# Hyena's tiles over n1 read four and two ahead, begun after a longer delay, with a larger share of the merge

## The chip, the core and the metric

One core of one Trainium2 chip runs the whole program. The metric is device time of one execution in microseconds. The core has five engines with queues of their own: PE (matmuls, with PEld for its weight loads), DVE, ACT, POOL and SP. SP does no arithmetic here; it issues nearly all DMAs, one after another.

## The reference, cut to what matters

Two sequences (512 and 2048 rows of width 1024) go through one layer of an encoder. Its inner width is divided into three branches: an mLSTM, a retention and a Hyena. The Hyena branch is what the change touches:

```python
def long_conv(u, spec, skip):
    l = u.shape[1]
    y = jnp.fft.irfft(jnp.fft.rfft(u, n=2 * l, axis=1) * spec[None], n=2 * l, axis=1)[:, :l]
    return y + u * skip

def hyena_branch(hy_in, hy_z, conv_w, conv_b, spec, skip):
    u = centred_conv3(hy_in.astype(f32), conv_w.astype(f32), conv_b.astype(f32))
    v, x1, x2 = u[..., :HY_WIDTH], u[..., HY_WIDTH:2 * HY_WIDTH], u[..., 2 * HY_WIDTH:]
    z = x1 * long_conv(v, spec[:, 0], sk[0])
    z = x2 * long_conv(z, spec[:, 1], sk[1])
    return z * jax.nn.silu(hy_z.astype(f32))
```

## The kernel before, in words

**Stages.** `front` normalises the rows, and starts the projections and the Hyena filters. Then one merge runs two streams side by side: the Hyena chain `stage_a0`, `freq(0)`, `inv_a(0)`, `freq(1)`, `inv_a(1)`, and the chain `projections`, `retention`. Then come `mlstm` and `final`.

**The Hyena chain.** A long convolution is a Fourier transform split in two steps, over n1 and over n2. `stage_a` is the step over n1: two matmuls (line 921) on one tile read from DRAM (`X`, line 790), two copies on ACT (924) and two stores into `Sg` (925). `stage_a0` does it for 20 tiles (4 of the short sequence, 16 of the long one). `freq(o)` is the step over n2 for 20 pairs of frequencies: matmuls of lines 948 and 983, products on DVE and POOL, results into `Z`. `inv_a(o)` is the inverse step over n1, 20 tiles again. Its `load` reads two tiles of `Z` (line 890), `load_x` reads a tile of the second factor `X` (and for o = 1 a tile of the gate `hyg`) in two halves of 64 partitions each (790), `mid` does two matmuls (1028), a product on DVE (1029) and, for o = 1, a product on POOL (1033) and two stores into `ymix` (1036). For o = 0 `back` passes the product to `stage_a` instead. All these tiles come from one pool, `hb`, of 18 buffers of 128x512 f32 (256 KB).

**The order.** Each stream is a Python generator that emits instructions and yields `(cost, due, pe)`. `merge` takes, of the streams that are due, the one with the smallest sum of costs divided by its weight; `self.now` moves on by the PE cost. `lag(cost, lag)` says that the stream isn't due again before its own cost and `lag` more have gone by. So a weight sets the share, and a lag holds a stream back at least so long. The sums are in planned us. The program is built with `schedule_with_timeline_sim=True`: the framework takes the emitted order as the priority, and from a model of time of its own settles the order of each engine's queue, in which one instruction may pass another. On the chip each queue then runs in that order.

**Beside it.** Line 544 is the projection of Hyena and mLSTM columns, line 554 that of retention and of gates; 376 to 378, 675, 680 and 693 make the filters; 1681 to 1702 and 1639 are retention. `RtHead` of head 3 is the last of the second stream. `before_mlstm` splits the first weights of the mLSTM; line 512 reads weights, line 348 takes their maximum on DVE.

Of the kernel before, what the change touches and what calls it, by code (L numbers as in the profile page):

```python
# [38 lines left out]
LF, LA, LI, LT, W1, W2, W3, LN, LM = 2.7, 1.0, 4.2, 1.6, 0.8, 1.08, 1.03, 1.5, 3.5  # L39
# [4 lines left out]
def geo(L):  # L44
    N = 2 * L
    N1 = N // 64
    V = N1 // 2
    return dict(N=N, N1=N1, K1=N1 // 2, V=V, GF=128 // N1, GS=128 // V, NTF=N // 128, NTS=L // 128)
# [105 lines left out]
class Trunk:  # L154
# [62 lines left out]
    def run(self):  # L217
        tc = self.tc
        with ExitStack() as ctx:
            self.psum = ctx.enter_context(tc.tile_pool(name="psum", bufs=8, space=PSUM))  # L220
            self.dram = ctx.enter_context(tc.tile_pool(name="dram", bufs=1, space=DRAM))
            self.cp = ctx.enter_context(tc.tile_pool(name="cp", bufs=1))
            self.setup()
            with ExitStack() as c1:
                self.hp = c1.enter_context(tc.tile_pool(name="hp", bufs=1))
                self.wp = c1.enter_context(tc.tile_pool(name="wp", bufs=2))
                self.hT = [[self.T(self.hp, [128, 8, 512], "h", F16, bufs=10) for i in range(2)] for b in range(5)]
                self.filter_pool = ExitStack()
                self.drain(self.front())
                with tc.tile_pool(name="hy", bufs=2, side="right") as self.hy:  # L230
                    self.load_ai()
                    self.drain(self.merge((self.chain(self.stage_a0(), self.freq(0), self.inv_a(0), self.freq(1), self.inv_a(1)), 275 * W3),
                                          (self.chain(self.projections(), self.retention()), 848)))
                self.drain(self.mlstm())
                with tc.tile_pool(name="fin", bufs=2, **TW) as self.fin:
                    self.final()
# [659 lines left out]
    def stage_a0(self):  # L896
        seq = [(L, j) for L in (LP, LS) for j in range(geo(L)['NTS'])]
        st = {}

        def load(i):  # L900
            L, j = seq[i]
            st[i] = self.hx(0, L, j)

        n = len(seq)
        load(0)
        load(1)
        for i in range(n + 1):
            if i:
                L, j = seq[i - 1]
                self.stage_a(L, 0, j, st.pop(i - 1))  # L910
            if i + 2 < n:
                load(i + 2)
            yield self.lag(0.86, 1.5)

    def stage_a(self, L, o, j, t):
        nc = self.nc
# [92 lines left out]
    def inv_a(self, o):  # L1009
        nc = self.nc  # L1010
        seq = [(L, j) for L in ((LS, LP), (LP, LS))[o] for j in range(geo(L)['NTS'])]
        zs, xs, st = {}, {}, {}

        def load(i):
            L, j = seq[i]
            zs[i] = [self.hb(self.Z[L, o][:, geo(L)['NTS'] * h + j::2 * geo(L)['NTS'], :]) for h in range(2)]

        def load_x(i):
            L, j = seq[i]
            g = self.in_halves(self.half_rows(self.hyg, L, j)) if o == 1 else None  # L1020
            xs[i] = self.hx(o + 1, L, j), g

        def mid(i):
            L, j = seq[i]
            z, (x, g) = zs.pop(i), xs.pop(i)
            ps = self.ps()
            for h in range(2):
                nc.tensor.matmul(ps[64 * h:64 * h + 64], self.ai[L][:, 128:192], z[h], start=True, stop=True)  # L1028
            nc.vector.tensor_tensor(out=x, in0=x, in1=ps, op=ALU.mult)
            if o == 0:  # L1030
                st[i] = x
            else:
                nc.gpsimd.tensor_tensor(out=g, in0=g, in1=x, op=ALU.mult)
                rows = self.half_rows(self.ymix[:, 1024:1536], L, j)
                for h in range(2):
                    nc.sync.dma_start(rows[h], g[64 * h:64 * h + 64])

        def back(i):
            L, j = seq[i]
            self.stage_a(L, 1, j, st.pop(i))  # L1040

        n = len(seq)
        load(0)
        yield self.lag(0.0, 5.0)
        for i in range(-1, n + 1):
            if o == 0 and i >= 1:
                back(i - 1)
            if 0 <= i < n:
                mid(i)
            if i + 1 < n:  # L1050
                load_x(i + 1)
            if i + 2 < n:
                load(i + 2)
            yield self.lag(1.71 if o == 0 else 0.86, LI)

    def gates(self):
        nc, I, tc = self.nc, self.I, self.tc
# [678 lines left out]
```

## Time and profile before

| | |
|---|---|
| time, median of 3 runs | 2651.07 us (2650.94 to 2654.84) |
| the profiled execution | 2648.68 us, span 2646.9 us |
| PE busy | 2557.2 us, 97% of the span |
| DVE, ACT, POOL busy | 51%, 40%, 19% |
| DMA | 321 MB, 39.8% of the 16 engines' time on SP's queue |
| mean granted TensorE clock | 0.988 |

PE is busy nearly all the time, so what can be won lies in the few stretches where it waits or where its clock is halved (a granted clock of 0.5 is 1.2 GHz, 1.0 is 2.4 GHz). An instruction's start is given from the span's start.

### The profile page before, as it was taken

To read this page: it belongs to the slowest core of one execution; us is meant where nothing else is said; L and a number is where in the kernel's file an instruction comes from. 1 tells how busy PE (TensorE), PEld (TensorE's weight loads), DVE (VectorE), ACT (ScalarE), POOL (GpSimd) and SP (SyncE) were. 2 spreads that over 40 slices of the span, in tenths; PEclk is the share of its full clock that TensorE was granted. 3 is DMA by queue.
4 is the path that set the end of the run, shared out by engine and by line. 5 is a ranking of instruction groups with operands and counts; after the bars stand their busy time and mean duration, and the time that the engine had idled before them with its cause. 6 is when DMAs were issued, how large, how long until landed. Compare 5 with 4: busy or idle time off the path is not lost.

```text
span 2646.9 us, 45607 instructions
## 1 busy us (share of the span) xinstructions
PE 2557.2 (97%) x17830; PEld 1770.2 (67%) x17830; DVE 1338.3 (51%) x3070; ACT 1053.7 (40%) x2030; POOL 493.9 (19%) x647
## 2 busy tenths in 40 slices
PE   7999979999999999999999979999999999899998
PEld 5565543444446777777777747787887777788887
DVE  6875635665554434545444444565556645522222
ACT  6455646442233333423333323555445545411111
POOL 0103312331011122322232341111111111100000
PEclk9999989999999999999999989999999999999999
DMA  6233377564454665434333782222121322322331
GB/s 207 84 99 108 98 220 252 167 187 127 126 160 128 207 198 160 126 100 132 116 104 97 226 228 65 52 66 61 37 64 42 89 73 59 133 102 95 111 104 48
DMA packets 238049, 321.30 MB, mean 121 GB/s; under 512 B 22755, under 2 KB 125947, under 8 KB 237833
## 3 DMA queue, kind: packets, MB, share of 16 engines
q1 hardware_dynamic: 237752, 318.11, 39.8%
q8 instruction: 141, 2.31, 0.4%
q14 instruction: 76, 0.61, 0.1%
q0 software_dynamic: 80, 0.26, 0.0%
HBM read 205.41 MB, written 112.89 MB: 120 GB/s over the span
## 4 chain that ended last, share of the span: by engine, by line
PE 78%; DMA 6%; ACT 4%; DVE 4%; issue 1%; SPq 1%; POOL 1%; DVEq 0%; POOLq 0%; ACTq 0%
PE ps L554 27%; PE ps L544 13%; PE ps L1287 13%; PE ps L948 6%; DMA rb<-rowd 3%; PE ps L983 3%; PE ps L1028 2%; PE ps L921 1%; PE ps L1639 1%; DMA wraw<-in_w_in 1%; PE ps L693 1%; PE ps L1438 1%; PE ps L1275 1%; PE ps L1698 1%; PE ps L846 1%
## 5 line engine op out<-in xcount | busy, mean ns | idle before, releaser
L554 PE MATMUL ps<-whi,h 128*128 128x256 f16 (+2 forms) x6080 | 913.7, 256 | 0.0
L554 PEld LDWEIGHTS <-h 128*128 128x128 f16 x9120 | 776.0, 98 | 150.0 <-issue 69.5
L554 PE MATMUL ps<-wlo,h 128*128 128x256 f16 (+2 forms) x3040 | 734.6, 256 | 0.0
L544 PE MATMUL ps<-h,whi 128*128 128x512 f16 x1600 | 484.9, 383 | 4.0 <-ACT whi L526 4.0
L544 PE MATMUL ps<-h,wlo 128*128 128x512 f16 x800 | 305.0, 381 | 0.0
L544 PEld LDWEIGHTS <-whi 128*128 128x128 f16 x1600 | 151.1, 99 | 212.8 <-issue 63.0
L1287 PE MATMUL ps<-h,yh 128*128 128x512 f32 x760 | 210.6, 396 | 1.6 <-ACT yh L369 1.6
L948 PE MATMUL ps<-hb,cB 128*64 128x512 f32 x640 | 165.9, 605 | 0.2 <-DMA hb<-F 0.2
L1287 PEld LDWEIGHTS ps<-h,yh 128*128 128x128 f32 x760 | 141.6, 188 | 33.7 <-ACT yh L369 1.9
L668 POOL TENSOR_TENSOR acc<-acc,win 128x512 f32<-128x512 f32 x80 | 107.2, 1340 | 201.4 <-ACT win L667 196.2
L544 PEld LDWEIGHTS <-wlo 128*128 128x128 f16 x800 | 78.7, 98 | 94.7 <-issue 4.9
L1618 POOL TENSOR_TENSOR m<-raw,tb 128x256 f32<-128x256 f32 x80 | 72.3, 904 | 336.2 <-ACT raw L1615 273.2
L1287 PE MATMUL ps<-h,yl 128*128 128x512 f32 x380 | 120.9, 395 | 0.0
L1615 ACT ACTIVATE raw<-ps,winv 128x256 f32<-128x256 f32 x80 | 37.8, 473 | 167.5 <-PE ps L554 98.9
L662 DVE TENSOR_TENSOR f<-ps,win 128x512 f32<-128x512 f32 x80 | 55.0, 688 | 88.7 <-PE ps L378 66.1
L813 DVE SCALAR_TENSOR_TENSOR cv<-u,sw,cv 128x512 f32<-128x512 f32 x120 | 98.1, 838 | 1.1
L527 DVE SCALAR_TENSOR_TENSOR wlo<-wraw,wsc,whi 128x512 f16<-128x512 f32 (+2 forms) x116 | 82.6, 749 | 22.8 <-ACT whi L526 21.6
L1637 ACT ACTIVATE vw<-va,rtv 128x128 f32<-128x128 f32 x144 | 51.9, 398 | 100.4 <-PE ps L1639 100.0
L948 PEld LDWEIGHTS ps<-hb,cB 128*64 128x64 f32 x640 | 41.5, 136 | 73.2 <-issue 60.6
L348 DVE TENSOR_REDUCE wam<-wraw 128x1 f32<-128x2048 f32 (+2 forms) x29 | 60.0, 2069 | 60.0 <-DMA wraw<-in_w_in 60.0
L1343 DVE TENSOR_TENSOR xt<-xt,ps 128x512 f32<-128x512 f32 x40 | 25.8, 684 | 126.9 <-PE ps L1287 126.9
L971 POOL TENSOR_TENSOR hb<-hb,hb 128x512 f32<-128x512 f32 x40 | 50.9, 1273 | 185.5 <-DVE hb L970 176.3
(318 smaller groups left out, 4045.8 us busy)
## 6 DMA issues: line engine op xcount, KB each, us to landing
F<-fo SPq DMA_DIRECT2D x160, 128.0 KB, 2.4
Sg<-hb SPq DMA_DIRECT2D x80, 256.0 KB, 2.3
hb<-F SPq DMA_DIRECT2D x80, 256.0 KB, 4.3
hb<-Sg SPq DMA_DIRECT2D x80, 256.0 KB, 5.1
Z<-hb SPq DMA_DIRECT2D x80, 256.0 KB, 3.5
hb<-Z SPq DMA_DIRECT2D x80, 256.0 KB, 3.7
rb<-rowd SPq DMA_DIRECT2D x80, 256.0 KB, 5.1
wraw<-in_w_in SPq DMA_DIRECT2D x36, 512.0 KB, 5.8
```

Source lines behind the costliest of these rows:

```text
L348: self.nc.vector.tensor_reduce(am[:, 0:1], src, axis=AX.XY if len(src.shape) == 3 else AX.X, op=ALU.max, apply_absolute_value=True)
L527: v = nc.vector.scalar_tensor_tensor(lo[:, k], raw[:, k], s, hi[:, k], op0=ALU.mult, op1=ALU.subtract)
L544: nc.tensor.matmul(out, w[x][:, k, wc:wc + 128], self.hT[b][y][:, k], start=(k == 0 and i == 0), stop=(k == 7 and i == 2))
L554: nc.tensor.matmul(out, self.hT[b][x][:, k, c * 128:(c + 1) * 128], w[y][:, k, wc:wc + n], start=(k == 0 and i == 0), stop=(k == 7 and i = ...
L662: nc.vector.tensor_tensor(out=f, in0=ps, in1=win, op=ALU.mult)
L668: nc.gpsimd.tensor_tensor(out=acc, in0=acc, in1=win, op=ALU.add)
L813: nc.vector.scalar_tensor_tensor(d, u[:, t:t + 512], w(t), d, op0=ALU.mult, op1=ALU.add)
L948: nc.tensor.matmul(ps[half[h]], Cs[i][:, 128 * h + 64 * r:128 * h + 64 * r + 64], src[h], start=True, stop=True)
L983: nc.tensor.matmul(pz[h], c[half[h], 256 + 128 * r:384 + 128 * r], y[r][half[h]], start=(r == 0), stop=(r == 1))
L1028: nc.tensor.matmul(ps[64 * h:64 * h + 64], self.ai[L][:, 128:192], z[h], start=True, stop=True)
L1287: self.nc.tensor.matmul(self.pss[n], a[p], w[q][:, n * 512:(n + 1) * 512], start=(k == 0 and i == 0), stop=(k == 11 and i == 2))
L1618: nc.gpsimd.tensor_tensor(out=m, in0=raw[:, :, ::-1], in1=sin[:, c:c + 2], op=ALU.mult)
```

## The change

The Hyena's weight in the merge goes from 275 to 295 (times 1.03). `stage_a0` reads four tiles before the first and stays four ahead (before: two), is first due after 9.0, and its tiles cost 1.0 with a lag of 0.5 (before: 0.86 and 1.5). `inv_a` reads two whole tiles first, `Z` and the factors, stays two ahead with both (before: `Z` two ahead, the factors one), is first due after 7.0 (before: 5.0 and then an empty round of its own cost and lag), and its tiles cost 1.0 or 2.0 with a lag of 1.5 (before: 0.86 or 1.71 with 4.2). In a round of `inv_a(0)` `mid` and the loads now come ahead of `back`. No instruction is added or taken out.

```diff
-  self.drain(self.merge((self.chain(self.stage_a0(), self.freq(0), self.inv_a(0), self.freq(1), self.inv_a(1)), 275 * W3),
+  self.drain(self.merge((self.chain(self.stage_a0(), self.freq(0), self.inv_a(0), self.freq(1), self.inv_a(1)), 295 * W3),
                         (self.chain(self.projections(), self.retention()), 848)))
...
         n = len(seq)
-        load(0)
-        load(1)
-        for i in range(n + 1):
-            if i:
-                L, j = seq[i - 1]
-                self.stage_a(L, 0, j, st.pop(i - 1))
-            if i + 2 < n:
-                load(i + 2)
-            yield self.lag(0.86, 1.5)
+        for i in range(4):
+            load(i)
+        yield self.lag(0.0, 9.0)
+        for i in range(n):
+            L, j = seq[i]
+            self.stage_a(L, 0, j, st.pop(i))
+            if i + 4 < n:
+                load(i + 4)
+            yield self.lag(1.0, 0.5)
...
         n = len(seq)
-        load(0)
-        yield self.lag(0.0, 5.0)
-        for i in range(-1, n + 1):
+        for i in range(2):
+            load(i)
+            load_x(i)
+        yield self.lag(0.0, 7.0)
+        for i in range(n + 1):
+            if i < n:
+                mid(i)
+            if i + 2 < n:
+                load(i + 2)
+                load_x(i + 2)
             if o == 0 and i >= 1:
                 back(i - 1)
-            if 0 <= i < n:
-                mid(i)
-            if i + 1 < n:
-                load_x(i + 1)
-            if i + 2 < n:
-                load(i + 2)
-            yield self.lag(1.71 if o == 0 else 0.86, LI)
+            yield self.lag(1.0 if o else 2.0, 1.5)
```

## Rows read from the trace of the kernel before

**Rows 1.** Windows by stage: length, PE, PEld, DVE, ACT, POOL busy, clock, DMA, GB/s

```profile
362.00:456.00 94.00, 83.18 (x354) 34.17 (x358) 43.15 (x71) 51.04 (x88) 17.78 (x25) 0.91 0.75 241
456.00:872.00 416.00, 414.68 (x2574) 200.78 (x2567) 222.39 (x430) 151.29 (x265) 82.17 (x124) 1.00 0.51 152
872.00:1019.00 147.00, 147.00 (x1099) 104.05 (x1098) 60.71 (x159) 59.28 (x134) 33.24 (x32) 1.00 0.66 208
1019.00:1465.00 446.00, 445.06 (x3365) 323.06 (x3366) 207.90 (x522) 151.41 (x338) 125.31 (x114) 1.00 0.36 113
...
1540.00:1567.00 27.00, 22.65 (x123) 13.38 (x122) 15.00 (x33) 6.21 (x16) 12.89 (x11) 0.94 0.83 235
1567.00:1592.00 25.00, 13.95 (x31) 3.65 (x31) 4.22 (x14) 1.50 (x4) 4.79 (x4) 0.73 0.65 182
```

**Rows 2.** PE's timeline where the merge begins: start, us, instruction, idle before

```profile
353.57 0.61 PE L544 MATMUL ps<-h,whi 128*128 128x512 f16 x2
...
358.55 0.38 PE L544 MATMUL ps<-h,wlo 128*128 128x512 f16 x1
367.07 3.78 PE L921 MATMUL ps<-hb,ai 64*128 64x512 f32 x8 [8.14 <-DMA hb<-X]
370.78 1.02 PE L675 MATMUL ps<-acc,ones 128*1 128x512 f32 x2
371.73 1.05 PE L680 MATMUL ps<-ones,acc 128*128 128x1 f32 x8
372.71 1.13 PE L921 MATMUL ps<-hb,ai 64*128 64x512 f32 x4
...
386.48 0.80 PE L376 MATMUL ps<-w,hd 128*128 128x512 f32 x1 [4.11 <-ACT w L369]
```

**Rows 3.** SP's timeline there: issues of DMAs

```profile
362.64 0.83 SPq L779 DMA_DIRECT2D ai<-c_AI  x2
363.51 3.81 SPq L790 DMA_DIRECT2D hb<-X  x6
```

**Rows 4.** PE's waits from 1540 to 1592

```profile
PE ps L1028 <- DMA hb<-Z: 11.1, 3, 4.8
PE ps L1700 <- DVE cf L1643: 2.9, 1, 2.9
PE ps L1698 <- DVE pt L1691: 0.8, 1, 0.8
PE ps L1689 <- ACT qkT L1682: 0.7, 1, 0.7
```

**Rows 5.** PE's timeline at the end of the merge

```profile
1550.11 1.88 PE L1028 MATMUL ps<-hb,ai 128*64 128x512 f32 x4
...
1553.44 1.07 PE L1028 MATMUL ps<-hb,ai 128*64 128x512 f32 x2
...
1560.24 1.08 PE L1028 MATMUL ps<-hb,ai 128*64 128x512 f32 x4
1561.67 1.08 PE L1028 MATMUL ps<-hb,ai 128*64 128x512 f32 x4
...
1563.99 1.07 PE L1028 MATMUL ps<-hb,ai 128*64 128x512 f32 x2
...
1566.86 0.49 PE L1700 MATMUL ps<-cf,qw 128*128 128x128 f32 x2
1570.53 1.73 PE L1028 MATMUL ps<-hb,ai 128*64 128x512 f32 x4 [3.19 <-DMA hb<-Z]
1577.06 3.44 PE L1028 MATMUL ps<-hb,ai 128*64 128x512 f32 x4 [4.80 <-DMA hb<-Z]
1583.57 1.94 PE L1028 MATMUL ps<-hb,ai 128*64 128x512 f32 x2 [3.06 <-DMA hb<-Z]
...
1591.11 1.07 PE L1028 MATMUL ps<-hb,ai 128*64 128x512 f32 x2
```

**Rows 6.** Windows: all of 1471 to 1540 and 1465 to 1567, then line 1028 alone

```profile
1471.00:1540.00 69.00, 69.00 (x550) 53.18 (x548) 37.81 (x83) 22.76 (x58) 34.49 (x29) 1.00 0.86 248
...
1465.00:1567.00 102.00, 97.65 (x725) 71.92 (x723) 55.03 (x121) 31.21 (x78) 48.32 (x42) 0.98 0.84 242
...
1465.00:1540.00 75.00, 12.94 (x44) 2.36 (x44) 1.00 0.85 245
```

**Rows 7.** SP's timeline in the last stage, 1471 to 1540: first, some, last

```profile
1471.59 2.17 SPq L790 DMA_DIRECT2D hb<-X  x2
...
1475.42 0.45 SPq L790 DMA_DIRECT2D hb<-hyg  x1
1476.68 1.10 SPq L1036 DMA_DIRECT2D ymix<-hb  x2
1477.84 0.59 SPq L790 DMA_DIRECT2D hb<-hyg  x1
1478.48 1.24 SPq L790 DMA_DIRECT2D hb<-X  x2
1479.76 1.06 SPq L890 DMA_DIRECT2D hb<-Z  x2
1480.92 1.09 SPq L790 DMA_DIRECT2D hb<-hyg  x2
1482.11 1.18 SPq L1036 DMA_DIRECT2D ymix<-hb  x2
...
1538.44 3.65 SPq L790 DMA_DIRECT2D hb<-hyg  x2
```

**Rows 8.** Windows 1552 to 1567: all instructions, then line 1028 alone

```profile
1552.00:1567.00 15.00, 13.53 (x69) 7.46 (x70) 8.60 (x23) 2.70 (x6) 9.40 (x8) 1.00 0.76 214
...
1552.00:1567.00 15.00, 6.45 (x16) 1.16 (x16) 1.00 0.76 214
```

## The prediction

> **What bounds the kernel now.** I read the busy shares first: PE is busy 97% of the span, no other engine above 51%, so time goes only where PE stands still or runs at half clock. The windows by stage then show which parts of the merge lose anything [rows 1]: from 456 to 1465 us, that is in both `freq` stages and in `inv_a(0)`, PE is busy all but 2 us of 1009; what is lost lies at the two ends. In 362 to 456 (`stage_a0`) PE is busy 83.2 of 94 us at a clock of 0.91; from 1540 to 1592 (the end of `inv_a(1)`) 36.6 of 52 us, at 0.94 and then 0.73. PE's waits and its timeline name the places. At the start the first tile of `stage_a0` stands in PE's queue ahead of its data: PE ends its line 544 at 358.9 and waits 8.1 us for `X` [rows 2], which SP could not issue before 363.5 [rows 3]; a second wait of 4.1 us for filter weights follows at 386. At the end retention's last matmul starts at 1566.86, and three Hyena tiles are left with nothing beside them [rows 5]: three waits for `Z`, 11.1 us in all, and 4.4 us of other waits just before [rows 4].
>
> **The change part by part.** No instruction is added or removed; everything is order, so the cost of each part is what PE waits.
>
> *Start of `stage_a0`.* Before, the Hyena's stream is due again after 0.86 + 1.5, and the second stream emits three or four pieces of line 544 (1.28 planned each, 6 matmuls) first: the 24 matmuls that I see in 5.4 us from 353.57 [rows 2]. With `lag(0.0, 9.0)` eight pieces come first (7 make 8.96, just short), 48 matmuls, at the same pace 10.8 us: PE reaches the first tile at 364.3. Its data can't be there sooner than now, 367.07: its loads are still the first that SP issues, after `ai`. 2.8 us of the wait stay, unless filter work (lines 675 and 680, 2.0 us, which now stand behind the first two tiles) comes ahead of it too. At stake are 8.1 us and the half clock behind the wait: the 8 matmuls took 3.78 us where two groups of 4 at full clock take 2.26, so 1.5 us. I take 8.1 − 2.8 + 1.2 = **6.5 us won**; bounds 0 (the queue's order stays) and 9.6. The two loads more in front are four issues at 0.6 us on SP [rows 3], ahead of stores that nothing waits for in this stage; at nothing, and 2.4 us later for the filter weights behind them if it is not so.
>
> *The second wait there.* 4.1 us for `fo<-in_hy_w`, whose issue stands behind stage-A loads and stores on SP. Later tiles leave SP freer, more loads fill it. Taken as unchanged; bounds 4.1 won, 2.4 lost.
>
> *Middle.* Planned sums: `stage_a0` goes from 21 x 0.86 = 18.1 to 20.0, each `freq` stays at 102.6 (1.71 + 20 x 3.42 + 19 x 1.71), `inv_a(0)` goes from 22 x 1.71 = 37.6 to 21 x 2.0 = 42. In `inv_a(0)` a tile now comes each 2.0 x (1 + 848/303.85) = 7.6 planned us instead of 6.8. PE doesn't wait there at all [rows 1], with less read ahead and a faster pace. Nothing, ± 2 us. The cover is line 554, and without it a tile would wait 3 to 5 us as at the end [rows 4].
>
> *When `inv_a(1)` begins.* Before, the sum ahead of it is 18.1 + 205.2 + 37.6 = 260.9 of a weight of 283.25, that is 0.921, and the second stream stands at 0.921 x 848 = 781. After: 20 + 205.2 + 42 = 267.2 of 303.85, 0.879, and the second stream stands at 746. So 35 us more of retention lie beside the last stage. Between 1465 and 1567 PE had 97.7 us of work [rows 6], 18.4 of it on 17 Hyena tiles at 1.08 [rows 5], so 79 us of retention; it becomes 114 us.
>
> *Its pace.* Before, `LI` holds a tile back 0.86 + 4.2 planned us, and what I see is 11 tiles in 69 us, 6.3 us each, without one wait of PE [rows 6]. After, the lag (2.5) no longer binds; the share does: 848/303.85 = 2.8 us of retention between tiles, 3.9 us with the tile's own 1.08. The 20 tiles are emitted with 56 us of retention between them, and some 55 us of retention remain behind the last one. So the three lonely tiles go.
>
> *What that wins.* From 1567.35 to 1591.11 PE did two and a half tiles (2.7 us) and 17 matmuls of line 544 (3.7 us at the pace of rows 2): 6.4 us of work in 23.8, so 17.4 us lost, 11.1 of them waits and the rest half clock. From 1540 to 1567 4.4 us of waits, and a clock of 0.94, that is 12% of 27 us at half speed, at most 1.6 us. **23.4 us at stake.** The largest of the small waits (2.9) followed a weight load that came slowly through the loaded queues.
>
> *What it costs.* A tile needs eight issues on SP: 1.06 + 1.09 + 1.24 + 1.18 = 4.6 us [rows 7]; SP's rows that start in those 69 us are 98 issues, 88 of them the Hyena's, and add up to 61.5 us (what SP waits within a row counted) [rows 7], 5.6 us a tile with retention's own. PE's queue would ask for a tile each 3.9 us. Lower bound: no wait, as now [rows 6]. Upper bound: 20 x (5.6 − 3.9) = 34 us. Nearest row: between 1550 and 1564 five tiles stand in PE's queue some 3.5 us apart, fed by loads that had run ahead, and PE waited 1.5 us there, for none of them [rows 4, 5]: 0.3 us a tile, 6 us for 20. The order in SP's queue also shows that it isn't the emitted one: a store slips in between the two halves of one `hyg` load, and `Z` and `hyg` of the fourth tile stand ahead of the second tile's store [rows 7]. Where loads are behind in the framework's model, PE's queue should get retention's matmuls first. With 2 us for the clock I take **8 us**.
>
> For this stretch the Trainium skill, Trace Analysis, "What DMA-bound means", has a rule that speaks against the change: a solid track of DMA slices on the issuing engine is descriptor generation, and such a stretch is bound by the issuing. Here SP issues 89% of the time while PE waits for nothing, so the trace bears it out only half; by the rule the sum below ends between 1 won and 11 lost, by the rows it ends at 18.6 won.
>
> *Retention's last block alone.* From 1552 to 1567 PE was busy 13.5 of 15 us [rows 8], 6.5 of it in line 1028. If the mLSTM's first matmuls don't fill that place, 6.5 us stand open; if they do, none. I take half, **3.3 us**.
>
> Sum: −6.5 − 23.4 + 8 + 3.3 = **−18.6 us**. The profiled execution took 2648.7 (its span 2646.9 and 1.8 around it), 2.4 below the median of the runs. 2651.1 − 18.6 gives **2633 us**.
>
> **The rivals.**
> - *All of it goes.* No new wait, nothing open behind retention, the filter weights early too: −9.6 − 4.1 − 23.4 = −37, 2614 us. For it: PE never waits in rows 6. Against: SP is nearly full there.
> - *The change doesn't do what it says at the start.* The framework settles the queues itself, and it already put the first tile ahead of data that came 8 us late. Then only the end is won: −23.4 + 8 + 3.3 = −12, 2639 us.
> - *SP paces the last stage.* PE's queue is in order, and retention's matmuls behind a late tile wait with it. If tiles stand 3.9 us apart and come each 5.0 (4.6 and a little of retention's issues), PE waits 1.1 us a tile, 22 us; with 6.5 behind retention that is −29.9 + 28.5: 2650 us, no change.
> - *The same, and slower.* At 5.6 us a tile the waits are 34 us: −29.9 + 40.5 = +11, 2662 us. It decides from (29.9 − 6.5)/20 = 1.2 us of wait a tile on. For it: 89% of issuing at 6.3 us a tile; deeper reading can shift, not shorten, 160 issues. Against: until retention ends there are 114 + 22 = 136 us, and 20 x 5.6 + 10 to start are 122; PE's order has only to follow.
>
> **How the numbers follow.** The forecast's case 0.54 (2622 to 2644), all of it 0.10, only the end 0.11, SP's pace without change 0.14, slower 0.11. 0.2% is 5.3 us, about what a measurement of this kernel can tell from no change. Faster (below 2645.8): 0.53 + 0.10 + 0.10 = 0.73; slower (above 2656.4) 0.12; the same 0.15. The range leaves out most of the first rival and the last: 2617 to 2655.
>
> **What would show it.** Step one: the wait for `X` before the first line 921 falls from 8.1 to under 3 us, with twice the line 544 ahead of it. Step two: the last line 1028 starts before retention's last matmul (1639 to 1702), and the three waits for `Z` with a clock of 0.5 are gone. Step three: in `inv_a(1)` PE's waits for `Z` add up to under 8 us. The prediction is wrong if they come to over 20 us, spread over the 20 tiles, or if a similar gap opens between retention and the mLSTM.

## The result and the profile after

The median went from 2651.0 to 2685.4 us (four runs each: 2649.0 to 2654.8 before, 2682.1 to 2692.1 after), a ratio of 1.013 with an interval of 1.011 to 1.015: slower, where 2633 us was forecast. The profiled execution took 2686.9 us with a span of 2685.1, that is 38.2 more than the span of before. Behind the new loop of `inv_a` the numbers of lines are one higher after (1639 is 1640).

The windows by stage of the kernel after; columns as in [rows 1]:

```profile
365.00:460.00 95.00, 84.37 (x354) 34.09 (x354) 43.18 (x73) 52.64 (x91) 19.82 (x25) 0.93 0.79 248
460.00:857.00 397.00, 395.34 (x2369) 181.81 (x2370) 216.35 (x405) 145.44 (x254) 73.28 (x117) 1.00 0.52 155
857.00:1000.00 143.00, 143.00 (x1058) 100.31 (x1057) 54.27 (x150) 53.12 (x119) 32.18 (x31) 1.00 0.65 201
1000.00:1436.00 436.00, 433.62 (x3281) 314.25 (x3278) 207.14 (x506) 154.35 (x345) 122.05 (x111) 1.00 0.38 119
1441.00:1556.00 115.00, 98.36 (x531) 53.96 (x529) 33.88 (x84) 17.11 (x45) 39.02 (x34) 0.94 0.81 234
1556.00:1600.00 44.00, 44.00 (x401) 40.87 (x402) 21.95 (x57) 16.33 (x38) 17.95 (x16) 1.00 0.18 47
1600.00:1640.00 40.00, 31.03 (x230) 21.78 (x229) 17.88 (x60) 15.26 (x32) 8.07 (x17) 0.87 0.30 69
```

Up to 1436 little has changed. The last stage (its 20 tiles stand from 1441.5 to 1555.4; 1471.2 to 1591.6 before) is where PE now loses: 98.4 us busy of 115, at a clock of 0.94, over the whole stage and not at its end. In 1556 to 1600 retention runs alone, at full speed, with the DMA engines 0.18 busy. In 1600 to 1640 retention's last blocks and the mLSTM's start stand with nothing beside them: 9 us idle, clock 0.87.

PE's waits from 355 to 1640 (us in total, times, longest):

```profile
PE ps L1028 <- DMA hb<-Z: 16.6, 7, 4.4
PE ps L921 <- ACT u L800: 5.4, 1, 5.4
PE ps L376 <- ACT w L369: 5.0, 1, 5.0
PE ps L1411 <- ACT kT L1400: 2.8, 1, 2.8
PE ps L1682 <- DVE qN L1622: 2.5, 3, 1.3
```

The wait for `X` [rows 2] is gone, with another of 5.4 us in its place, for ACT's `u`. The three lonely waits for `Z` [rows 4] have become seven within the stage, 16.6 us instead of 11.1. PE's timeline shows a second thing there:

```profile
1456.40 1.07 PE L1028 MATMUL ps<-hb,ai 128*64 128x512 f32 x2
1458.58 1.07 PE L1028 MATMUL ps<-hb,ai 128*64 128x512 f32 x2 [1.11 <-DMA hb<-Z]
1460.93 1.99 PE L1028 MATMUL ps<-hb,ai 128*64 128x512 f32 x4 [1.28 <-DMA hb<-Z]
1466.24 1.07 PE L1028 MATMUL ps<-hb,ai 128*64 128x512 f32 x2 [3.32 <-DMA hb<-Z]
1467.24 0.40 PE L554 MATMUL ps<-whi,h 128*128 128x256 f16 x1
1467.43 0.42 PE L554 MATMUL ps<-wlo,h 128*128 128x256 f16 x1
```

A tile is two matmuls of line 1028 (x4 in the rows; one alone is x2). Side by side the two took 1.08 us together at full clock [rows 5]; alone each takes 1.07. In the last stage 26 matmuls now stand alone, before 7. Behind the wait of 3.3 us line 554 runs at the lower of the clock's two levels, with 0.40 us for a matmul that takes 0.27 at the higher. Line 1028 grew from 52.1 to 64.9 us busy, its waits by 5.5, line 554 by 2.3 us: some 21 of the 38 us. Line 554, all its matmuls taken together over the whole span (they overlap, so its `whi` and `wlo` rows can't be added), and the grouped row of line 1028, after:

```profile
0.00:2686.00 2686.00, 925.41 (x9120) 777.75 (x9120) 0.99 0.40 120
...
L1028 PE MATMUL ps<-hb,ai 128*64 128x512 f32 x160 | 64.9, 629 | 16.6 <-DMA hb<-Z 16.6
```

and before:

```profile
0.00:2647.00 2647.00, 923.11 (x9120) 776.03 (x9120) 0.99 0.40 121
...
L1028 PE MATMUL ps<-hb,ai 128*64 128x512 f32 x160 | 52.1, 646 | 11.1 <-DMA hb<-Z 11.1
```

### The profile page after: what moved, and what is told of

Same layout as the page of the kernel before. It is cut to its first block, busy times and chain, and to the rows that moved or that the text cites. A ratio compares the mean times of both kernels' runs of the same rounds, so it can differ in the third digit from the quotient of the medians.

```text
span 2685.1 us, 45590 instructions
## 1 busy us (share of the span) xinstructions
PE 2582.3 (96%) x17830; PEld 1777.0 (66%) x17830; DVE 1333.3 (50%) x3070; ACT 1055.1 (39%) x2030; POOL 493.6 (18%) x647
## 4 chain that ended last, share of the span: by engine, by line
PE 39%; DMA 5%; DVE 3%; ACT 2%; SPq 1%; issue 1%; POOL 1%; DVEq 0%; POOLq 0%; ACTq 0%
PE ps L554 13%; PE ps L1288 12%; PE ps L544 5%; DMA rb<-rowd 3%; PE ps L1028 1%; DMA wraw<-in_w_in 1%; PE ps L1439 1%; PE ps L1276 1%; PE ps L948 1%; PE ps L1511 1%; DVE t L1467 1%; DMA hb<-Z 1%; ACT y L1204 1%; PE ps L1535 1%; PE ps L1538 1%
## 5 line engine op out<-in xcount | busy, mean ns | idle before, releaser
L811 DVE TENSOR_SCALAR cv<-u,sw 128x512 f32<-128x512 f32 x60 | 34.8, 581 | 109.8 <-ACT u L800 94.3
```

## The experiments

The theory (A): the new lag of 1.5 asks PE for a tile each 3.9 us, faster than its five pieces of 256 KB (two `Z`, `X`, `hyg`, the store) can move; PE's ordered queue then stands, the clock falls, and tiles come apart into two matmuls alone. Rivals: (B) the larger share itself is what costs, since it leaves retention's end uncovered; (C) the new `stage_a0` is the loss; (D) SP's issuing sets the pace, as the prediction's slow rivals had it; later (E) the 18 buffers, and (F) the loop of a store that waits for GpSimd with the next loads behind it on SP.

All results; the last stage is worked out from PE's rows in each trace (first to last matmul of line 1028, per tile; PE's matmuls behind the first of them up to the last, which tells how much other work went on, since line 1028's own 79 are among them in every run; waits for `Z`; matmuls of a tile alone), GB/s from a window over the stage. Each ratio is to runs of the kernel before made beside it:

| kernel | median us | ratio, interval | us per tile | matmuls in stage | waits for Z | alone | GB/s |
|---|---|---|---|---|---|---|---|
| before | 2651.0 | | 6.34 | 696 | 11.1 | 7 | |
| after | 2685.4 | 1.013 [1.011, 1.015] | 5.99 | 523 | 16.6 | 26 | 234 |
| e1_share | 2645.9 | 0.999 [0.998, 1.000] | 6.23 | 925 | 2.0 | 2 | |
| e2_a0 | 2654.9 | 1.002 [1.001, 1.004] | 6.18 | 636 | 15.3 | 3 | |
| e3_inva | 2676.4 | 1.011 [1.009, 1.013] | 5.87 | 540 | 13.8 | 26 | |
| e4_pair | 2676.4 | 1.011 [1.009, 1.013] | 5.51 | 515 | 25.1 | 0 | 250 |
| e5_lag | 2639.8 | 0.997 [0.996, 0.998] | 6.37 | 951 | 0 | 0 | 240 |
| e6_act | 2680.4 | 1.012 [1.009, 1.015] | 5.77 | 479 | 13.5 | 19 | 240 |
| e7_lag3 | 2663.5 | 1.006 [1.003, 1.008] | 6.31 | 688 | 10.6 | 25 | |
| e8_deep | 2667.3 | 1.007 [1.005, 1.010] | 5.40 | 521 | 9.5 | 28 | 261 |
| e9_noa0 | 2635.9 | 0.995 [0.993, 0.997] | 6.06 | 913 | 0 | 2 | 237 |
| e11_hb20 | 2680.2 | 1.011 [1.009, 1.013] | 6.03 | 523 | 16.6 | 26 | 235 |
| e12_nohyg | 2663.4 | 1.005 [1.004, 1.007] | 5.00 | 503 | 7.1 | 25 | 226 |
| e13_deep20 | 2669.1 | 1.007 [1.006, 1.009] | 5.41 | 521 | 9.4 | 28 | |
| e14_store | 2675.8 | 1.011 [1.009, 1.013] | 5.58 | 519 | 12.1 | 24 | 252 |
| e15_deepst | 2676.4 | 1.010 [1.008, 1.012] | 5.71 | 523 | 14.6 | 24 | |
| e16_read | 2668.9 | 1.007 [1.006, 1.009] | 6.27 | 593 | 17.4 | 5 | |
| e17_285 | 2655.1 | 1.002 [1.001, 1.003] | 6.35 | 827 | 0.7 | 4 | 236 |
| e18_nohyg3 | 2653.0 | 1.002 [1.001, 1.004] | 4.47 | 513 | 0 | 26 | 251 |
| e19_zonly | 2654.2 | 1.002 [1.001, 1.003] | 4.36 | 489 | 0.1 | 27 | 195 |

Not every expectation below came true. e1_share came out 4 us above its range and e7_lag3 just above its own; e2_a0, e8_deep and e14_store fell between their two ranges; e15_deepst, e16_read and e17_285 came out above both, and e19_zonly's time between its two, with 27 matmuls alone where few were expected.

### One part of the change alone

```diff
e1_share, on before
-  self.inv_a(1)), 275 * W3),
+  self.inv_a(1)), 295 * W3),
e2_a0, on before: the new loop of stage_a0 alone
e3_inva, on before: the new loop of inv_a alone
```

> The kernel before with the weight 295 alone. Theory A (after a change of pace the last stage asks for tiles faster than SP issues their loads; that costs waits for Z and splits each tile's two matmuls): the share alone keeps the slow pace (lag 4.2), so no waits for Z over 3 us in sum in the last stage, nearly all pairs of line 1028 together, its last tile before retention's end: 2630 to 2642 us. Theory B (the larger share itself hurts, because it leaves retention's last blocks and the mLSTM's start uncovered): 2660 to 2675 us.

> The kernel before with the new stage_a0 alone. Theory A: this part is not what made the kernel slower; the wait for X of 8.1 us before the first tile is replaced by one of about 5 us for ACT's u (as in the changed kernel), so 2642 to 2652 us. Rival (the start's part is a share of the loss): 2655 us or more.

> The kernel before with the new inv_a alone (weight 275, old stage_a0). Theory A: 40 matmuls of line 1028 in the last stage, over 20 of them alone, waits for Z of 15 us or more: 2665 to 2680 us. Theory B: without the share no gap behind retention, so 2645 to 2655 us.

The share alone gains some 4 us, at the edge of what the runs tell apart (the interval ends at 1.000); it costs nothing, so B falls: with it the last stage begins at 1429 and PE waits 2.0 us for `Z`. The new `stage_a0` alone costs some 5 us (2 to 9 by the interval), so it isn't where 34 went; C falls. In its trace, which is that of its slowest run (2665.2 us), the wait for `X` is replaced, not removed:

```profile
PE ps L921 <- ACT u L800: 7.1, 1, 7.1
PE ps L376 <- ACT w L369: 5.5, 1, 5.5
```

The new `inv_a` alone costs 26 us.

### The lag

```diff
e5_lag, on after (e7_lag3: 3.0 in place of 1.5)
-            yield self.lag(1.0 if o else 2.0, 1.5)
+            yield self.lag(1.0 if o else 2.0, LI)
```

> The changed kernel with inv_a's lag back at 4.2 instead of 1.5 (share, stage_a0 and the deeper reading stay). Theory A: the last stage lasts as long as before in matmuls (about 780 between its first and last), waits for Z under 4 us, pairs together, its end at retention's end: 2630 to 2642 us. Theory B: 2665 to 2680 us, since the share stays.

> The changed kernel with a lag of 3.0 in inv_a (1.5 there, 4.2 before): tiles of the last stage asked for each 5 us or so, about what SP needs for one (4.9). Pace theory: between the two, waits for Z 2 to 8 us, part of the pairs apart, 2645 to 2662 us. Rival (the length of the lag as such does nothing, only the kernel's other order): no trend, over 2675 us or under 2642 us.

`LI` is 4.2. With it everything else of the change stays, and the time goes some 46 us down, below that of before; with 3.0 it lies between. Windows of e5_lag, the last stage and what follows:

```profile
1441.00:1560.00 119.00, 117.45 (x942) 90.28 (x940) 61.19 (x142) 34.96 (x86) 56.36 (x49) 1.00 0.81 240
1560.00:1600.00 40.00, 30.76 (x217) 20.69 (x218) 21.45 (x65) 14.54 (x29) 11.04 (x19) 0.87 0.39 99
```

The DMA engines do there what they do in after (0.81, 240 beside 234 GB/s) and the stage is about as long; but 942 matmuls start in it instead of 531 in the windows shown, because PE isn't held. Every tile's two matmuls stand together:

```profile
1503.55 1.08 PE L1028 MATMUL ps<-hb,ai 128*64 128x512 f32 x4
...
1510.41 1.08 PE L1028 MATMUL ps<-hb,ai 128*64 128x512 f32 x4
```

Line 1028's busy time is 44.1 us, 20.8 below that of after; with the 16.6 us of waits and 3.9 of line 554 that makes 41.3 of the 47.5 us between the two spans:

```profile
0.00:2638.00 2638.00, 921.51 (x9120) 775.72 (x9120) 0.99 0.40 122
...
L1028 PE MATMUL ps<-hb,ai 128*64 128x512 f32 x160 | 44.1, 618 | 0.0
```

### Tiles apart

```diff
e4_pair, on after: the second half of Z is loaded first
-  zs[i] = [self.hb(...) for h in range(2)]
+  zs[i] = [self.hb(...) for h in (1, 0)][::-1]
```

> The changed kernel, but each tile's two loads of Z are issued in the other order, so that the half that the first matmul reads comes last and the two matmuls can stand together. Theory A: line 1028's time in the last stage falls from 40.8 to 21 to 24 us; if the waits for Z stay at about 17 us, 2672 to 2677 us. Rival (the split is only a sign that SP is late): the 12 us come back as longer waits for Z, 2682 to 2688 us.

The first matmul in PE's order now waits for the load that lands last, so no matmul stands alone, line 1028's busy time falls to 47.1 us, and the waits rise to 25.1. The waits were expected to stay. The net is 9 us. Being apart thus costs time of its own, but mending it leaves the larger part of the loss.

### What sets the pace

```diff
e6_act, on after: X and hyg of inv_a(1) by ACT's queue
-            g = self.in_halves(self.half_rows(self.hyg, L, j)) if o == 1 else None
-            xs[i] = self.hx(o + 1, L, j), g
+            queue = nc.scalar if o == 1 else None
+            g = self.in_halves(self.half_rows(self.hyg, L, j), queue) if o == 1 else None
+            xs[i] = self.hx(o + 1, L, j, queue), g
e14_store, on after: the store by ACT's queue
-                    nc.sync.dma_start(rows[h], g[64 * h:64 * h + 64])
+                    nc.scalar.dma_start(rows[h], g[64 * h:64 * h + 64])
e8_deep, on after: i + 3 for i + 2 in inv_a, three tiles in front
e15_deepst: e8_deep and e14_store
e11_hb20, on after: HB = 20; e13_deep20: e8_deep with HB = 20
```

> The changed kernel with the four loads of X and hyg of each tile of inv_a(1) issued by ACT instead of SP, so that SP issues 4 of 8 DMAs of a tile. If SP's issuing sets the pace (157 issues of 0.55 us and 13 us behind stores in 115 us): PE's waits for Z fall from 16.6 to under 6 us, 2645 to 2665 us. Rival (the 16 DMA engines, busy 0.81 of that stretch, or the way of the data set it): waits stay at 14 to 18 us, 2678 to 2690 us.

> The changed kernel with inv_a reading three tiles ahead instead of two (same 18 buffers). Pace theory: deeper reading only puts off the first late tile by some 5 us; waits for Z 10 to 17 us, 2673 to 2690 us. Rival (what is missing is depth, the loads are asked for too late): waits under 5 us, 2645 to 2662 us.

> The kernel after with 20 instead of 18 buffers for the Hyena's tiles. Buffers set the pace (a Hyena tile holds four of them from its load to its store's landing): 5.99 x 18/20 = 5.4 us per tile in the last stage, fewer waits, 8 to 15 us faster than after (2670 to 2677). The transfers themselves set it (0.81 of the DMA engines busy): the pace stays within 0.15 of 5.99 and the time within 5 us of after (2680 to 2690).

> Reading three tiles ahead in inv_a as in e8_deep (2667.3), with 20 buffers. Buffers set the pace: 5.4 becomes 4.9 us per tile, waits under 5 us, time 2655 to 2662. Transfers set it: pace 5.3 to 5.5 and time 2663 to 2671.

> The kernel after with the Hyena's stores of inv_a(1) issued by ACT's queue, so that no load stands behind a store that waits for GpSimd. If the loop store, next loads, landing, product sets the pace (two tiles in 12 us), it goes from 5.99 to 5.0 to 5.4 us per tile, the waits for Z fall from 16.6 to under 9 us and the time by 12 to 25 us (2660 to 2673). If the transfers themselves set it, the pace stays at 5.8 to 6.0, the waits over 13 us and the time within 6 us of after.

> Reading three tiles ahead (e8_deep, 5.40 us per tile, 2667.3) and the stores by ACT's queue. If the loop still sets the pace at three tiles ahead, 4.8 to 5.1 us per tile and 2655 to 2662 us; if the transfers are the floor there (0.85 of the DMA engines busy at 5.40), 5.3 to 5.5 us per tile and 2663 to 2671 us.

D falls for the kernel after: e6_act leaves SP about half of the issuing (80 issues and 37.5 us between 1441 and 1556, where after has 157 and 85.7), and the tiles come each 5.77 us, with 13.5 us of waits. Its own side effect clouds the price a little, since ACT's computing then stands behind its loads. The Trainium skill, Perfetto Trace Analysis, "What DMA-bound means", which the prediction weighed, would call a stretch with a solid issuing track bound by the issuing; by e6_act this one isn't. E falls with the stores on SP: two buffers more change neither pace, nor waits, nor time beyond the uncertainty, with two tiles ahead or three.

F is borne out in part. Reading a tile further ahead helps most: 18 us, and the transfers reach 261 instead of 234 GB/s; and SP's own waits show what the third tile takes away. Over the last stage SP's queue stands at the store of line 1036, behind GpSimd's product, in after, e8_deep, and the later e12_nohyg and e18_nohyg3 (us in total, times, longest):

```profile
SPq L1036 <- POOL hb L1033: 12.9, 11, 5.2
SPq L1036 <- POOL hb L1033: 0.6, 1, 0.6
SPq L1036 <- POOL hb L1033: 22.4, 19, 3.2
SPq L1036 <- POOL hb L1033: 9.8, 8, 3.5
```

The longest wait in after shows the loop. The two halves of one tile start 5.8 us apart, GpSimd's product follows the second, SP's store follows the product, and no load is issued from 1488.8 until then; the DMA engines nearly stop, at 35 GB/s from 1491 to 1496:

```profile
1484.96 1.94 PE L1028 MATMUL ps<-hb,ai 128*64 128x512 f32 x2 [4.36 <-DMA hb<-Z]
1490.76 1.19 PE L1028 MATMUL ps<-hb,ai 128*64 128x512 f32 x2
1492.80 1.27 POOL L1033 TENSOR_TENSOR hb<-hb,hb 128x512 f32<-128x512 f32 x1 [8.36 <-DVE hb L1029]
1494.10 1.10 SPq L1036 DMA_DIRECT2D ymix<-hb  x2
1491.00:1496.00 5.00, 5.00 (x32) 2.87 (x31) 0.69 (x1) 0.00 (x0) 1.27 (x1) 1.00 0.16 35
```

Taking the stores off SP gives 0.4 us a tile with two tiles read ahead (and some 10 us of time, with intervals that overlap), and with three ahead nothing more: 5.71 us a tile in its profile, which is of its slowest run, beside 5.40 in e8_deep, and 2676.4 beside 2667.3 us with intervals that overlap. There another wait takes the loop's place: SP's loads stand 23.0 us behind stores of `ymix` that have to land before their buffers are free. The stores by ACT together with more buffers were not run.

```diff
e12_nohyg, on after: no load of hyg; e18_nohyg3: the same, three tiles ahead
...
-                nc.gpsimd.tensor_tensor(out=g, in0=g, in1=x, op=ALU.mult)
+                g = self.hb()
+                nc.gpsimd.tensor_tensor(out=g, in0=x, in1=x, op=ALU.mult)
e19_zonly, on e12_nohyg: no load of X in inv_a(1) either, x = self.hb(),
  and adds in place of both products there
```

> The kernel after without the load of the gate hyg: GpSimd squares x into a fresh buffer in its place, so the Hyena's output lacks the gate. Per tile four loads and stores of 256 KB and six DMAs instead of five and eight; the count of buffers is unchanged. Transfers set the pace: 5.99 x 4/5 = 4.8 us per tile, waits for Z under 8 us. Buffers set it: the pace stays between 5.4 and 6.0 and the waits between 9 and 17 us. If asking early is what costs (tiles each alone, half clock), the time falls only as far as the waits do: 2660 to 2675.

> e12_nohyg (no load of the gate hyg, GpSimd squares x in its place) and three tiles read ahead. If what is left at 5.00 us per tile is the loop over two tiles (10 us), 4.0 to 4.4 us per tile, waits for Z under 3 us, 2640 to 2652 us. If it is the transfers and their issuing, 4.8 to 5.1 us per tile, waits 5 to 8 us, 2656 to 2666 us.

> The kernel after without the loads of hyg and of X in inv_a(1): the output lacks gate and product, adds to fresh buffers stand in their place. Three transfers of 256 KB and four DMAs per tile instead of five and eight, read two tiles ahead as in after. If transfers and issues set the pace, the asked pace is met: 3.9 to 4.3 us per tile, waits under 3 us, few matmuls of a tile alone, 2635 to 2650 us. If the loop over two tiles sets it, 4.8 to 5.2 us per tile and waits of 5 to 9 us, 2658 to 2668 us.

Windows over the last stage, e12_nohyg first:

```profile
1436.00:1531.00 95.00, 87.93 (x506) 48.95 (x505) 34.44 (x81) 15.21 (x40) 32.83 (x32) 0.98 0.80 226
```

e8_deep:

```profile
1440.00:1542.00 102.00, 92.54 (x521) 50.81 (x520) 31.64 (x78) 14.67 (x39) 36.65 (x32) 0.97 0.89 261
```

e18_nohyg3:

```profile
1438.00:1523.00 85.00, 85.00 (x517) 49.16 (x516) 33.70 (x82) 15.98 (x43) 32.30 (x32) 1.00 0.85 251
```

and e19_zonly, with the two stretches behind it:

```profile
1438.00:1521.00 83.00, 82.90 (x492) 46.16 (x490) 34.88 (x80) 14.91 (x39) 32.48 (x32) 1.00 0.69 195
1521.00:1566.00 45.00, 45.00 (x407) 41.28 (x406) 23.95 (x58) 16.87 (x40) 19.70 (x18) 1.00 0.12 34
1566.00:1610.00 44.00, 35.77 (x260) 25.68 (x258) 18.26 (x61) 16.73 (x36) 8.11 (x18) 0.84 0.32 76
```

In these three kernels the Hyena's output lacks the gate, in the last one also the product with `X`. A fifth of a tile's bytes less, and a quarter of its issues, takes the pace from 5.99 to 5.00 at two tiles ahead and from 5.40 to 4.47 at three. But the two steps don't mean the same. In e18_nohyg3 PE waits for no tile, at a clock of 1.00, so 4.47 us is what PE's order asks, and so is the 4.36 of e19_zonly. In e12_nohyg, with the same bytes as e18_nohyg3, the tiles come each 5.00 us at 226 GB/s while SP stands 22.4 us behind its stores: there the loop over two tiles holds them, and not the bytes, as my expectation of e18_nohyg3 had it. e19_zonly, with the loop of after and three fifths of the bytes, runs without a late tile although SP stands 31.3 us behind its stores, so what the loop costs hangs on how long the transfers behind it take.

With three tiles ahead and all five pieces, in e8_deep, the loop is gone from SP's queue and PE still waits 9.5 us. The DMA engines are then 0.89 busy, and SP's issues add up to 84 of 102 us. Which of the two holds the 5.40 us isn't shown, since every run with fewer bytes also had fewer issues. Either puts the 3.9 us asked for out of reach here: a tile is 1.31 MB, 5.0 us at 261 GB/s, and eight issues at e8_deep's mean of 0.54 us are 4.3 us, both before retention's own.

e19_zonly also parts the account. Its data are in time (waits 0.1 us, clock 1.00), yet 27 matmuls stand alone: other work stands between a tile's halves though nothing waits (line 1028 is 1027 there):

```profile
1454.86 0.27 PE L554 MATMUL ps<-whi,h 128*128 128x256 f16 x1
1455.06 1.07 PE L1027 MATMUL ps<-hb,ai 128*64 128x512 f32 x2
1456.07 0.28 PE L554 MATMUL ps<-whi,h 128*128 128x256 f16 x1
...
1456.83 1.07 PE L1027 MATMUL ps<-hb,ai 128*64 128x512 f32 x2
```

From after to e19_zonly 31 us go, and 32 to e18_nohyg3, which also has no late tile: late data, with the half clock behind it. From e19_zonly to e5_lag another 14 us go, and line 1028's busy time between these two differs by 58.4 − 44.1 = 14.3 us: tiles apart. Together they are the 46 us that one number in the lag is worth. Each of the two shares is as sure as the medians are, to some 5 us, and an estimate, since e19_zonly also has less to load than either kernel beside it.

### The share, and a version that beats both

```diff
e9_noa0, on e5_lag: the old stage_a0
e16_read: e9_noa0 with 275 * W3; e17_285: with 285 * W3
```

> The kernel after with the old lag LI in inv_a(1), and the old stage_a0. If the new stage_a0 costs time of its own (+5 us alone in e2_a0) and the rest is as in e5_lag (2639.8), 2634 to 2637 us. Rival: the new stage_a0 costs only where inv_a is the old one, since both only shift retention; then as e5_lag, 2638 to 2642.

> The kernel before with the new inv_a alone, but its lag LI, and the old share: e9_noa0 without the larger share. If reading ahead is what wins, 2636 to 2641 us, beside e9_noa0's 2635.9. If it is the share that wins (e1_share alone -4.2 us) and reading ahead only lets it, 2645 to 2652 us with lonely tiles at the end as before.

> e9_noa0 with a share of 285 instead of 295. In e9_noa0 retention's last state begins at 1568.7, 21 us behind the last Hyena tile, and PE was busy 18.9 of the 23 us from 1547 at a clock of 0.93. If that open end costs what a smaller share gives back, 2632 to 2635 us; if a share of 285 leaves Hyena tiles lonely again, 2637 to 2642 us.

e9_noa0 takes 2635.9 us, 0.995 of before (0.993 to 0.997), 4 us below e5_lag. Its windows:

```profile
1432.00:1548.00 116.00, 116.00 (x919) 88.19 (x916) 58.25 (x141) 31.73 (x79) 53.08 (x47) 1.00 0.80 237
1548.00:1600.00 52.00, 45.09 (x346) 32.70 (x345) 29.82 (x81) 19.25 (x42) 15.58 (x23) 0.90 0.42 109
```

PE is busy all of the last stage; what is left, 7 us and some half clock, lies where retention ends and the mLSTM begins. e16_read came out above both of its expectations, and e17_285 too: reading ahead without the larger share loses 19 us. The plan says why. With the new `inv_a` the Hyena's planned sum is 18.1 + 205.2 + 42 + 20 = 285.3, and a share of 275 is a weight of 283.25: its last tiles are planned behind the end of retention. In e16_read the last one starts at 1615.9, 41 us after retention's last state product, and PE's windows there are

```profile
1497.00:1576.00 79.00, 74.35 (x533) 54.19 (x535) 45.59 (x95) 22.82 (x54) 40.91 (x35) 0.96 0.84 243
1576.00:1617.00 41.00, 23.59 (x66) 7.41 (x63) 6.88 (x19) 1.51 (x4) 9.79 (x8) 0.67 0.73 216
```

With 285 the two streams end together (1586.5 and 1585.0), with 295 the Hyena 21 us earlier. Even where they end together one wait of 8.3 us for DVE's `qN` appeared in e17_285, so the open end is not the only thing that its 19 us to e9_noa0 hold.

## Why the prediction was wrong

- **What it costs** is the step that failed: 8 us for late tiles in the last stage, with "0.3 us a tile" from five tiles that stood 3.5 us apart [rows 5]. Those were fed by loads that had run ahead, as the text itself said; over 20 tiles there is no such store to live on. Measured: 16.6 us of waits, 0.8 us a tile (under the 20 named as the mark, and over the 8 of the third step), 5.6 us of half clock (busy time times what the clock lacks, in windows of 5 us), and 12.8 us more of line 1028's own time, in which part of that half clock is counted again. The bound of 34 was about what it came to, for another reason.
- **The missing term** is the tiles apart, some 14 us. [rows 5] already had it: x2 at 1.07 us beside x4 at 1.08. I counted each tile at 1.08 and passed over the singles, seven in the stage.
- **Its pace**, "the share does: 3.9 us per tile", was about right as what is asked for (4.36 and 4.47 where no tile was late) and wrong as what comes. A check that was left out is in [rows 6]: at the 248 GB/s of that stretch the 1.31 MB of a tile take 5.3 us. I priced SP's issues, and neither the bytes nor the stores that SP's loads stand behind.
- **The rivals** had the sign and the place (late tiles in PE's ordered queue, 2662 us) and the wrong reason: it was not the time of SP's issues, which e6_act halved for 0.2 us a tile, but with two tiles ahead SP's standing behind its stores, 12.9 us in after and 23.3 still in e6_act.
- **When `inv_a(1)` begins** and **what that wins** held: more of retention lies beside the stage, the lonely tiles at the end are gone, and with the old lag the larger share ends at 2640 to 2636 us, near the forecast for the whole.
- **Retention's last block alone** was sized at 3.3 us; 1600 to 1640 lost 9.0 us idle and 4.2 of half clock, where before lost 1.3 us in 1592 to 1625.
- **Start of `stage_a0`**: 6.5 us forecast; from 355 to 465 PE lost 14.1 idle and 6.0 in half clock before, 12.0 and 5.1 after, so 3 us were won there. The tile's data was not the only thing that came late: ACT's `u` ended last. As a part by itself it cost 5 us: in e2_a0 the last stage starts 14 us later. Its planned sum of 20.0 for 18.1 accounts for about half of that, 1.9 x (1 + 848/283.25) = 7.6 us.
- **Second wait** (4.1 to 5.0) and **middle** (from 465 to the last stage 2.1 us lost, then 3.6) were as forecast.

Of the 38 us, some 21 are those of lines 1028 and 554. Line 1411, the mLSTM's first transposes, has 4.9, busy time and waits together, but 5.1 in e5_lag too, so that isn't the lag's. The rest is spread over many lines and was not told apart. Whether transfers or issuing hold the 5.40 us with three tiles ahead stays open too.

## What to carry to other kernels

A planned lag is a demand on the transfers: before shortening it, divide the bytes of one tile by the rate that the stage already shows, and compare with the pace asked for. Look also at which queue its loads stand in: behind a store that waits for the tile's own product they come late by as much as the tile did. Where an ordered queue asks too early, the cost isn't only the wait but the clock behind it and whatever comes apart in the order; an idle-free stretch that asks more slowly does the same transfers with nearly twice the other work beside it. And a share of a merge is only right for the planned sum of the stream that it weighs: when a stage's planned time grows, the share has to grow too.

## What the runs showed of the hardware

Two matmuls of 128 rows onto 64 columns each, into different halves of the array, took 1.08 us together and 1.07 us each when other matmuls stood between them. The Trainium skill, TensorEngine Tiling (Array Packing), "Key Properties", says that different tiles of the array can execute matmuls in parallel; the rows agree, and add that a matmul of another shape in between (line 554, on the whole array) takes the whole of that gain. As a mean of the whole last stage the transfers never went over 261 GB/s in any window taken, at 0.78 to 0.89 of the DMA engines busy where all five pieces were moved, whichever queue issued them. That is no limit of the DMA engines: in e8_deep's stage single stretches of 5 us reach 315 GB/s.
